# Splitting the weights of the first MLP product by two transfers from GpSimd instead of by ScalarE and VectorE

## The chip, the cores and the metric

The kernel runs on one core of one Trainium2 chip. The metric is the device time of one execution in microseconds; three runs of the kernel before gave 783.15 to 783.79 us, with a median of 783.71 us. Lower is better.

The engines are named as in the profile: PE is TensorE (PEld its weight loads), DVE is VectorE, ACT is ScalarE, POOL is GpSimd, SP is SyncE, which here only issues transfers. Each engine works through its own queue of instructions in order; engines wait for one another with semaphores.

## The reference

One transformer block on 512 tokens of width 1024 in float32: a gated linear attention branch and a latent attention branch, merged, projected and added to the input, and then an MLP with a squared ReLU, whose inner width is 4096. The part that the change touches is the first product of the MLP.

```
h = h + merged @ w_out[l]
m = rmsnorm(h, g_mlp[l])
h = h + jnp.square(jax.nn.relu(m @ w_ff1[l])) @ w_ff2[l]
return rmsnorm(h, g_final)
```

Here `m` is 512 x 1024, `w_ff1` is 1024 x 4096 and `w_ff2` is 4096 x 1024.

## The kernel before

**The products.** TensorE reads float32r operands, which hold fewer bits than float32. To keep the precision, each operand is split into `hi`, the value rounded to float32r, and `lo`, the rest `x - hi`. A product is then three matmuls onto the same accumulator (`mm3`, lines 91 to 93): hi by hi, lo by hi and hi by lo.

**The first MLP product.** The 4096 columns of `w_ff1` are cut into 32 blocks of 128 columns. The block is called f00 to f07 in quarter 0 of the MLP, f10 to f17 in quarter 1, up to f37. One block is 8 tiles of 128 x 128, laid out in SBUF as 128 partitions x 1024 numbers (512 KB). `hidden` multiplies a block with the normed and transposed rows `mT` in 24 matmuls of 512 columns: for each of the eight `k`, two that read the block's `hi` and one that reads its `lo`.

**How a block comes in.** `weights` (line 221) loads the block in float32 into a staging tile `wf` with one transfer from SP, in pieces of 512 bytes; ACT copies it, rounded, into `wh` (line 96); DVE writes `wl = wf - wh` (line 97). There are three staging tiles, four `wh` and four `wl`; a new block takes the buffer of the fourth one before it, once its last reader is through. These four pairs are shared with the weights of the second product.

**The order within a quarter.** A quarter has eight blocks of the first product, then seven block products with the quarter's part of `w_ff2` in a Strassen-like scheme (`ORDER`: 1, 5, 6, 3, 7, 4, 2). Each of these uses two pairs of `wh` and `wl` (`b1` to `b7`), made by the same `split`. In the order of taking buffers, a quarter goes: six blocks f, two tiles b1, blocks f6 and f7, two tiles each of b5, b6, b3, b7, b4 and b2. So f10 and f11 of the next quarter follow into the buffers of b4, f12 and f13 into those of b2, f14 and f15 into those of f10 and f11, the tiles of b1 into those of f12 and f13, f16 and f17 into those of f14 and f15, and b5 into those of f16 and f17.

**After a block.** ACT applies the ReLU (`fa`, line 1015) and the squares (`px`, `qx`); `pair_units` makes from two blocks the sums and differences of the left side and splits them on ACT and DVE (`ga`, `gb`, `gc`, `gd`).

**What sets the order on each engine.** A planner built into the framework orders the instructions of each engine by costs and dependencies of its own; the program forces an order only in some places (`in_program_order`, `goes_behind`). The first four blocks f00 to f03 are handled separately (`early`, and the branch for `j in (2, 3)`), so that they fit into the transition from the normed rows. POOL has nothing to do in the MLP except the last normalisation and one transfer from its queue, the gains `gfin` (line 1137).

Of the kernel before, what the change touches and what calls it, by code (L numbers as in the profile page):

```python
# [14 lines left out]
AF = mybir.ActivationFunctionType  # L15
ALU = mybir.AluOpType
AX = mybir.AxisListType

P = 128
S = 512  # L20
NT = S // P
D = 1024
KD = D // P
DFF = 4096
# [35 lines left out]
def tile_block(ctx: ExitStack, tc: tile.TileContext, t, out: bass.AP):  # L60
    nc = tc.nc
# [5 lines left out]
    def tl(shape, dt, tag, bufs, name):  # L67
        serial[0] += 1
        return sb.tile(shape, dt, tag=tag, bufs=bufs, name=f"{name}_{serial[0]}")

    def u2(name, dt=F32, shape=(P, S)):
        return tl(list(shape), dt, "u2", 25, name)
# [7 lines left out]
    def ps(tag, name):  # L80
        serial[0] += 1
        return pp.tile([P, S], F32, tag=tag, bufs=4, name=f"{name}_{serial[0]}")
# [4 lines left out]
    def raw(x):  # L87
        return x.bitcast(F32)

    def mm3(acc, lh, ll, rh, rl, start, stop, onto=False):  # L90
        nc.tensor.matmul(acc, lh, rh, start=start, stop=False, skip_group_check=onto)  # L91
        nc.tensor.matmul(acc, lh, rl, start=False, stop=False, skip_group_check=onto)  # L92
        nc.tensor.matmul(acc, ll, rh, start=False, stop=stop, skip_group_check=onto)  # L93

    def split(hi, lo, src, rest=nc.vector):
        nc.scalar.activation(hi, src, AF.Copy)  # L96
        rest.tensor_tensor(lo, src, raw(hi), op=ALU.subtract)  # L97
# [12 lines left out]
    def traced():  # L110
        return len(nc.cur_bb.bb.instructions)
# [15 lines left out]
    def goes_behind(late, early, engines):  # L127

        ins = nc.cur_bb.bb.instructions
        for e in engines:  # L130
            a, b = [[i for i in ins[x:y] if i.engine == e] for x, y in (early, late)]
            if a and b:
                issued_after(b[0], a[-1].name)
# [78 lines left out]
    def stage(nk, nw, name):  # L212
        wf = tl([P, nk, nw], F32, "wf", 3, f"{name}f")
        return wf

    def halves(nk, nw, name):
        wh = tl([P, nk, nw], F32R, "wh", 4, f"{name}h")
        wl = tl([P, nk, nw], F32R, "wl", 4, f"{name}l")
        return wh, wl

    def weights(src, name):
        k, w = src.shape
        nk = k // P
        wf = stage(nk, w, name)
        nc.sync.dma_start(wf, src.rearrange("(k p) w -> p k w", p=P))
        wh, wl = halves(nk, w, name)
        split(wh, wl, wf)
        return wh, wl

    w_in = t["w_in"][0]  # L230

    def proj_begin(w, col, name, tag="mm"):
        wh, wl = weights(w[:, col : col + P], name)
        return wh, wl, ps(tag, name)

    def proj_run(begun, src, half=None, ks=range(KD)):
        wh, wl, acc = begun
        c = slice(0, S) if half is None else slice(half * 256, half * 256 + 256)
        for k in ks:
            mm3(acc[:, c], wh[:, k, :], wl[:, k, :], src[k][:, 0, c], src[k][:, 1, c], k == 0, k == KD - 1)  # L240
        return acc
# [89 lines left out]
    for k in range(KD):  # L331
        wh, wl = (vh[k // 2][x][:, k % 2, :] for x in range(2))
# [173 lines left out]
    def gla_v(pr):  # L506

        accs = [ps("mm", f"gv{pr}{i}") for i in range(NT)]
        col = C_GV + pr * S
        res = v_tiles(pr)  # L510

        def piece(i, k2, wh, wl):
            tok = slice(i * P, (i + 1) * P)
            for kk in range(2):
                k = 2 * k2 + kk
                mm3(accs[i], xT[k][:, 0, tok], xT[k][:, 1, tok], wh[:, kk, :], wl[:, kk, :], k == 0, k == KD - 1)

        kept = []
        for k2 in range(KD // 2):
            wh, wl = weights(w_in[k2 * 2 * P : (k2 + 1) * 2 * P, col : col + S], f"gv{pr}{k2}")  # L520
            if k2 >= 2:
                kept.append((k2, wh, wl))
                continue
            for i in range(NT):
                piece(i, k2, wh, wl)
        for i in range(NT):
            for k2, wh, wl in kept:
                piece(i, k2, wh, wl)
            v_evict(accs[i], res[i], i)
        return res  # L530
# [329 lines left out]
    def rows_product(lhs, w, nk, name, first_done, done, flip):  # L860
        for c in range(2):
# [11 lines left out]
            for k2 in range(nk // 2):  # L873
                wh, wl = weights(w[k2 * 2 * P : (k2 + 1) * 2 * P, c * S : (c + 1) * S], f"{name}{c}{k2}")
                if k2 >= nk // 2 - staggered:
                    kept.append((k2, wh, wl))
                    continue
                for i in range(NT):
                    piece(i, k2, wh, wl)
# [32 lines left out]
    mT = fm.out  # L912
    w1, w2 = t["w_ff1"][0], t["w_ff2"][0]
# [33 lines left out]
    FQ = DFF // P // NQ  # L947
# [55 lines left out]
    def hidden(qd, j):  # L1003

        if qd == 0 and j < 2:
            acc = early[j][2]
        elif qd == 0 and j in (2, 3):
            at = traced()
            begun = proj_begin(w1, j * P, f"f{qd}{j}")
            goes_behind((at, traced()), span["norm", NT - 1] if j == 2 else span["evacuate", 1], SPLITTERS)  # L1010
            acc = proj_run(begun, mT)
        else:
            acc = proj_run(proj_begin(w1, (qd * FQ + j) * P, f"f{qd}{j}"), mT)
        a = u2(f"fa{qd}{j}")
        nc.scalar.activation(a, acc, AF.Relu)  # L1015
        return a

    def pair_units(qd, p, a22):

        px, qx = u2(f"px{qd}{p}"), u2(f"qx{qd}{p}")  # L1020
        for x in range(2):
            a = hidden(qd, 2 * p + x)
            c = slice(x * HT, (x + 1) * HT)
            nc.scalar.activation(px[:, c], a[:, 0:HT], AF.Square)  # L1024
            nc.scalar.activation(qx[:, c], a[:, HT:S], AF.Square)
        a11, a12, a21, a22_ = px[:, 0:HT], px[:, HT:S], qx[:, 0:HT], qx[:, HT:S]
        y, z = u2(f"y{qd}{p}"), u2(f"z{qd}{p}")
        s1, s2, s3, s4 = y[:, 0:HT], y[:, HT:S], z[:, 0:HT], z[:, HT:S]
        g1 = u4(f"ga{qd}{p}")
        split(g1[:, 0, :], g1[:, 1, :], px)  # L1030
        nc.vector.tensor_tensor(s1, a21, a22_, op=ALU.add)
        nc.vector.tensor_tensor(s2, s1, a11, op=ALU.subtract)  # L1032
        nc.vector.tensor_tensor(s3, a11, a21, op=ALU.subtract)
        nc.vector.tensor_tensor(s4, a12, s2, op=ALU.subtract)
        h2, l2 = u2(f"gbh{qd}{p}", F32R), u2(f"gbl{qd}{p}", F32R)
        split(h2, l2, y)
        h3, l3 = u2(f"gch{qd}{p}", F32R), u2(f"gcl{qd}{p}", F32R)
        split(h3, l3, z)
        c4 = slice((p % 2) * HT, (p % 2 + 1) * HT)
        split(a22[:, 0, c4], a22[:, 1, c4], a22_)  # L1040
        lo, hi = slice(0, HT), slice(HT, S)
        return {1: (g1[:, 0, lo], g1[:, 1, lo]), 2: (g1[:, 0, hi], g1[:, 1, hi]),
                5: (h2[:, lo], l2[:, lo]), 6: (h2[:, hi], l2[:, hi]),
                7: (h3[:, lo], l3[:, lo]), 3: (h3[:, hi], l3[:, hi]),
                4: (a22[:, 0, c4], a22[:, 1, c4])}
# [148 lines left out]
```

## Time and profile before

| what | value |
|---|---|
| median of three runs | 783.71 us |
| the profiled execution | 783.52 us, of which the span is 781.8 us |
| PE busy | 772.8 us (99%) |
| DVE busy | 544.2 us (70%) |
| ACT busy | 410.1 us (52%) |
| POOL busy | 104.1 us (13%) |
| the MLP on the span | blocks f00 on from 444.6 us; each quarter some 82 us |

The span runs from the first to the last instruction; what lies around it is 1.7 us in the profiled execution. In the views, a row of a timeline starts with the instruction's start and its duration in microseconds, followed by its engine, line, operation and `out<-in`. Buffer numbers are left out of the names, so the tiles of b1, b5 and so on of one quarter all show as `b_10h`. A matmul's shown duration holds its passage through the array, so the starts of two matmuls in a row, not the duration, tell the rate. A group's row gives the busy time, the mean duration in nanoseconds and the idle time just before, with what ended it.

### The profile page before, as it was taken

To read this page: it belongs to the slowest core of one execution; us is meant where nothing else is said; L and a number is where in the kernel's file an instruction comes from. 1 tells how busy PE (TensorE), PEld (TensorE's weight loads), DVE (VectorE), ACT (ScalarE), POOL (GpSimd) and SP (SyncE) were. 2 spreads that over 40 slices of the span, in tenths; PEclk is the share of its full clock that TensorE was granted. 3 is DMA by queue.
4 is the path that set the end of the run, shared out by engine and by line. 5 is a ranking of instruction groups with operands and counts; after the bars stand their busy time and mean duration, and the time that the engine had idled before them with its cause. 6 is when DMAs were issued, how large, how long until landed. Compare 5 with 4: busy or idle time off the path is not lost.

```text
span 781.8 us, 10005 instructions
## 1 busy us (share of the span) xinstructions
PE 772.8 (99%) x3736; PEld 648.5 (83%) x3736; DVE 544.2 (70%) x839; ACT 410.1 (52%) x685; POOL 104.1 (13%) x168
## 2 busy tenths in 40 slices
PE   9999999999999999999999999999999999999996
PEld 7888888888888888888888898888888888888885
DVE  7767656576566449799973578874787578848695
ACT  7564624532562236798853366435553455436644
POOL 1023203213021314211120100000000000000014
PEclk9999999999999999999999999999999999999998
DMA  7634133133223411523033731155106411460002
GB/s 247 168 90 111 33 84 106 54 94 107 62 75 82 75 40 51 139 55 108 28 128 88 267 110 54 53 179 145 43 14 208 141 46 35 162 183 6 28 1 108
DMA packets 102385, 74.47 MB, mean 95 GB/s; under 512 B 14976, under 2 KB 86656, under 8 KB 102336
## 3 DMA queue, kind: packets, MB, share of 16 engines
q1 hardware_dynamic: 101248, 70.66, 31.4%
q10 hardware_dynamic: 864, 2.38, 0.8%
q0 software_dynamic: 224, 0.79, 0.3%
q8 instruction: 29, 0.48, 0.3%
q14 instruction: 20, 0.16, 0.1%
HBM read 69.62 MB, written 2.10 MB: 92 GB/s over the span
## 4 chain that ended last, share of the span: by engine, by line
PE 94%; issue 3%; DVE 2%; ACT 1%; POOL 0%; POOLq 0%
PE f L92 8%; PE f L93 7%; PE f L91 7%; PE gx L91 4%; PE gx L93 4%; PE gx L92 4%; PE gv L320 3%; PE gr L91 2%; PE gr L93 2%; PE wo L93 2%; PE wo L91 2%; PE gr L92 2%; PE gz L93 2%; PE za L92 2%; PE gz L91 2%
## 5 line engine op out<-in xcount | busy, mean ns | idle before, releaser
L962 DVE TENSOR_TENSOR w<-w,w 128x1024 f32<-128x1024 f32 x32 | 38.7, 1220 | 0.4
L1137 POOL DMA_DIRECT2D gfin<-in_g_final x1 | 0.7, 653 | 282.6 <-PE f L93 282.6
L744 ACT ACTIVATE e<-s,top 128x512 f32<-128x512 f32 x32 | 21.9, 685 | 6.0 <-DVE top L741 5.0
L909 DVE TENSOR_TENSOR h<-gx,h 128x512 f32<-128x512 f32 x32 | 21.5, 683 | 1.8 <-PE gx L93 1.7
L97 DVE TENSOR_TENSOR pT<-tp,pT 128x512 fp32r<-128x512 f32 x32 | 21.6, 678 | 0.5 <-ACT pT L96 0.4
L741 DVE TENSOR_REDUCE top<-s 128x1 f32<-128x512 f32 x32 | 21.6, 678 | 0.1
L96 ACT ACTIVATE pT<-tp 128x512 fp32r<-128x512 f32 x32 | 18.9, 593 | 3.1 <-PE tp L758 2.9
L758 PE MATMUL tp<-ident,e 128*128 128x128 f32 x128 | 19.2, 273 | 0.1
L91 PE MATMUL av<-pT,v 128*128 128x256 f32 x64 | 19.3, 301 | 0.0
L776 POOL TENSOR_TENSOR tb<-tb,g 128x512 f32<-128x512 f32 x8 | 11.1, 1383 | 56.9 <-DVE tb L775 43.8
L758 PEld LDWEIGHTS tp<-ident,e 128*128 128x128 f32 x128 | 15.3, 140 | 3.9 <-DVE pT L97 0.5
L535 DVE TENSOR_TENSOR za<-za,R 128x512 f32<-128x512 f32 x8 | 5.5, 691 | 18.7 <-PE za L93 18.7
L1015 ACT ACTIVATE fa<-f 128x512 f32<-128x512 f32 x32 | 18.5, 578 | 0.0
L92 PE MATMUL av<-pT,v 128*128 128x256 f32 x64 | 18.4, 288 | 0.0
L93 PE MATMUL av<-pT,v 128*128 128x256 f32 x64 | 18.1, 283 | 0.0
L96 ACT ACTIVATE gbh<-y 128x512 fp32r<-128x512 f32 x16 | 10.1, 634 | 14.0 <-DVE y L1032 14.0
L451 POOL TENSOR_TENSOR qk<-qkf,e3f 128x256 f32<-128x256 f32 x8 | 7.8, 973 | 63.8 <-DVE qkf L443 63.8
L91 PE MATMUL s<-kbuf,q 128*128 128x512 f32 x32 | 13.7, 429 | 0.3 <-DVE pT L97 0.3
L1024 ACT ACTIVATE px<-fa 128x256 f32<-128x256 f32 x32 | 13.4, 418 | 1.0
L96 ACT ACTIVATE b_20h<-w 128x1024 fp32r<-128x1024 f32 x7 | 7.4, 1059 | 12.1 <-PE gx L93 6.0
L96 ACT ACTIVATE b_10h<-w 128x1024 fp32r<-128x1024 f32 x7 | 7.4, 1059 | 12.1 <-PE gx L93 6.0
L96 ACT ACTIVATE b_00h<-w 128x1024 fp32r<-128x1024 f32 x7 | 7.4, 1058 | 12.1 <-PE gz L93 6.0
(1460 smaller groups left out, 2806.9 us busy)
## 6 DMA issues: line engine op xcount, KB each, us to landing
w<-in_w_ff SPq DMA_DIRECT2D x64, 256.0 KB, 3.4
x<-in_xt SPq DMA_DIRECT2D x8, 256.0 KB, 5.3
vw<-in_w_in SPq DMA_DIRECT2D x8, 256.0 KB, 5.4
q<-ro SPq DMA_DIRECT2D x16, 128.0 KB, 4.6
h<-in_x ACTq DMA_DIRECT2D x4, 512.0 KB, 4.9
out<-ms SPq DMA_DIRECT2D x7, 256.0 KB, 2.2
gr0f<-in_w_in SPq DMA_DIRECT2D x1, 512.0 KB, 5.6
za0f<-in_w_in SPq DMA_DIRECT2D x1, 512.0 KB, 6.5
```

The costliest lines, as they stand in the source:

```text
L91: nc.tensor.matmul(acc, lh, rh, start=start, stop=False, skip_group_check=onto)
L92: nc.tensor.matmul(acc, lh, rl, start=False, stop=False, skip_group_check=onto)
L93: nc.tensor.matmul(acc, ll, rh, start=False, stop=stop, skip_group_check=onto)
L96: nc.scalar.activation(hi, src, AF.Copy)
L97: rest.tensor_tensor(lo, src, raw(hi), op=ALU.subtract)
L320: nc.tensor.matmul(v_accs[i], a[:, i * P : (i + 1) * P], b, start=k == 0 and x == 0, stop=k == KD - 1 and x == 2)
L741: nc.vector.tensor_reduce(top, acc, axis=AX.X, op=ALU.max, negate=True)
L744: nc.scalar.activation(e, acc, AF.Exp, bias=top, accum_out=tot)
L758: nc.tensor.transpose(tp[:, k * P : (k + 1) * P], e[:, k * P : (k + 1) * P], ident)
L909: nc.vector.tensor_tensor(hc, acc, hc, op=ALU.add)
L962: nc.vector.tensor_tensor(wq[dst][g], wq[x][g], wq[y][g], op=op)
L1015: nc.scalar.activation(a, acc, AF.Relu)
```

## The change

For the 28 blocks from f04 on, `hidden` no longer calls `weights`. A new function makes `wh` and `wl` with two transfers issued by POOL and one ACT instruction. The first transfer reads the float32 block and writes it into the float32r tile `wh`, rounded on the way. ACT writes `-wh` into `wl`. The second transfer reads the same float32 block again and adds it to what stands in `wl`, so that `wl` becomes `w - wh`. The staging tile, the rounding copy on ACT and the subtraction on DVE are gone for these blocks. The blocks are laid out on the host so that each partition's 1024 numbers lie in one run of 4 KB.

```
-            acc = proj_run(proj_begin(w1, (qd * FQ + j) * P, f"f{qd}{j}"), mT)
+            name = f"f{qd}{j}"
+            wh, wl = weights_by_transfer(t["w1_blocks"][qd * FQ + j].rearrange("p (k f) -> p k f", k=KD), name)
+            acc = proj_run((wh, wl, ps("mm", name)), mT)
...
+    def weights_by_transfer(src, name):
+
+        wh, wl = halves(KD, P, name)
+        nc.gpsimd.dma_start(wh, src)
+        nc.scalar.activation(wl, raw(wh), AF.Copy, scale=-1.0)
+        nc.gpsimd.dma_start(wl, src, accum_op=ALU.add)
+        return wh, wl
...
+    arrays["w1_blocks"] = np.ascontiguousarray(
+        arrays["w_ff1"][0].reshape(KD, P, DFF // P, P).transpose(2, 1, 0, 3).reshape(DFF // P, P, D)
+    )
```

## The prediction

> **What bounds the kernel now.** I read the page first (parts 1 and 2), then busy times by stage, then single instructions of TensorE and ScalarE around one quarter of the MLP, then the transfers.
>
> ```profile
> span 781.8 us, 10005 instructions
> ...
> PE 772.8 (99%) x3736; PEld 648.5 (83%) x3736; DVE 544.2 (70%) x839; ACT 410.1 (52%) x685; POOL 104.1 (13%) x168
> ...
> PE   9999999999999999999999999999999999999996
> ...
> PEclk9999999999999999999999999999999999999998
> ```
> ```profile
> core 0: us, PE busy (x) PEld busy (x) DVE busy (x) ACT busy (x) POOL busy (x), PEclk, DMA share, GB/s
> ...
> 458.00:500.00 42.00, 42.00 (x187) 34.46 (x186) 33.02 (x48) 27.88 (x50) 0.00 (x0) 1.00 0.22 63
> 500.00:536.00 36.00, 36.00 (x161) 29.80 (x160) 25.45 (x30) 13.99 (x14) 0.00 (x0) 1.00 0.57 174
> ```
> PE is busy in every slice, and in the stages of the MLP it is busy the whole time (42.00 of 42.00 us) at full clock, with DVE and ACT below it and the transfers at 0.22 and 0.57 of their time. The MLP is bound by TensorE alone. The change takes no matmul away, so taking work from DVE, ACT or SP can bring nothing there; the only question is whether the new way of making the weights is late.
>
> ```profile
> 529.34 0.39 PE L91 MATMUL f<-mT,f10h 128*128 128x512 f32 x1
> ...
> 551.10 0.39 PE L91 MATMUL f<-mT,f14h 128*128 128x512 f32 x1
> ...
> 556.54 0.39 PE L91 MATMUL f<-mT,f15h 128*128 128x512 f32 x1
> ```
> From f14 to f15 are 24 matmuls in 5.44 us: 0.227 us each.
>
> ```profile
> 522.74 1.06 ACT L96 ACTIVATE f10h<-f10f 128x1024 fp32r<-128x1024 f32 x1 [3.02 <-DMA w<-in_w_ff]
> 524.10 1.06 ACT L96 ACTIVATE f11h<-f11f 128x1024 fp32r<-128x1024 f32 x1 [0.30 <-PE gx L93]
> 528.18 1.06 ACT L96 ACTIVATE f12h<-f12f 128x1024 fp32r<-128x1024 f32 x1 [3.02 <-PE gw L93]
> 529.54 1.06 ACT L96 ACTIVATE f13h<-f13f 128x1024 fp32r<-128x1024 f32 x1 [0.30 <-PE gw L93]
> ...
> 556.52 1.06 ACT L96 ACTIVATE f16h<-f16f 128x1024 fp32r<-128x1024 f32 x1 [0.74 <-PE f L92]
> ...
> 562.92 0.58 ACT L1015 ACTIVATE fa<-f 128x512 f32<-128x512 f32 x1
> ...
> 566.69 0.63 ACT L96 ACTIVATE gch<-z 128x512 fp32r<-128x512 f32 x1
> ```
> ```profile
> L97 DVE TENSOR_TENSOR f14l<-f14f,f14h 128x1024 fp32r<-128x1024 f32 x1 | 1.2, 1226 | 3.6 <-ACT f14h L96 3.6
> ```
> These rows show when a buffer comes free, since the split waits for that alone (its release is PE). Counted from f10's first matmul (T = 529.34), the buffer of f10 is free at -6.6, of f11 at -5.2, of f12 at -1.2, of f13 at +0.2 us. That of f16 comes free as f15 begins. A split then needs 1.06 + 1.23 us and fits each time, because the float32 block waits in a staging tile.
>
> **The change part by part.** Gone are 28 rounding copies on ACT (in their place 28 negating copies of the same shape, so 1.06 us each), 28 subtractions on DVE (28 x 1.23 = 34 us of an engine that is not the bound) and 28 issues on SP. All three lay beside PE: 0. What was hidden was the load itself; now the load may only start when the buffer `wh` is free, and the chain is buffer free, first transfer, ACT 1.06 us, second transfer, matmul. New on POOL are 56 transfers. The order of the changed kernel's instructions on POOL in quarter 1 is:
>
> ```
> f10h f11h f10l f12h f11l f13h f12l f14h f13l f14l f15h f15l f16h f16l f17h f17l
> ```
> ```profile
> gfin<-in_g_final POOLq DMA_DIRECT2D x1, 512.0 KB, 3.9
> pos_i<-in_positions POOLq DMA_DIRECT2D x1, 256.0 KB, 4.4
> ```
> ```profile
> wo12f<-in_w_out SPq DMA_DIRECT2D x1, 512.0 KB, 3.5
> ...
> f10f<-in_w_ff SPq DMA_DIRECT2D x1, 512.0 KB, 4.2
> ...
> f35f<-in_w_ff SPq DMA_DIRECT2D x1, 512.0 KB, 5.7
> ```
> ```profile
> w<-in_w_ff SPq DMA_DIRECT2D x64, 256.0 KB, 3.4
> ```
> ```profile
> L1065 POOL TENSOR_TENSOR ms<-h,gfin x4: 1292/1302/2162, 760.0 to 766.6; 128x512 f32<-128x512 f32 x4
> ...
> L1137 POOL DMA_DIRECT2D gfin<-in_g_final x1: 653/653/653, 732.3 to 732.3; - x1
> ```
> POOL is held 0.65 us by an issue of this shape. Call the first transfer's issue to landing `a`, the second's `c`. For `a`: between 3.5 (wo12f) and 5.7 (f35f, among other loads); nearest are gfin, the same shape from the same queue, at 3.9, and f10f at 4.2. I take 4.2; that rounding on the way costs more is not excluded. For `c` there is no adding transfer in the trace. It must read the block and the target: at least a plain 4.2, at most two plain ones in a row, 8.4. Twice the bytes (256 to 512 KB) went from 3.4 to 4.2, 0.8 us per 256 KB, so a second reading of 512 KB adds 1.7: I take c = 5.9. Ends kept: a + c from 7.0 to 12.8, taken 10.1.
>
> The Trainium skill, page "Collectives: The Full Stack", section "The bandwidth ceiling: the fold count and why AG ≠ RS ≠ AR", says that an adding transfer is slow by its two source reads on one ring, at half the rate, and not by the addition; doubling the whole landing by it would give c = 8.4 and a sum at the upper end below. No run here shows it yet.
>
> Handovers get 0.1 us (an allowance).
>
> *Start of quarters 1, 2, 3 (S1).* f10h issues at -6.6 and lands at a - 6.6; ACT is done at a - 5.44; f10l lands at a + c - 5.34, PE sees it at a + c - 5.24. Until then PE has only four matmuls (two of f10's `hi`, two of f11's), to 0.91. S1 = a + c - 6.15 = 3.95 us. f11l follows within f10's 5 us, and f12h, queued behind f10l, has f10 and f11 to hide under. f13l is queued behind f14h, which waits until f10 is through at c + 4.0; it lands at 2c + 4.6 and is needed at c + 14.85, late only from c = 10.3. f14 and f15 have three blocks (16 us) of lead.
>
> *f6 of each quarter, four times (S2).* Its buffer comes free as f15 begins (call it 0). f16l lands at a + c + 1.26, is seen at a + c + 1.36. PE has f15's 24 matmuls, two of f16 and nine of product 1 that the planner put there: 35 x 0.227 = 7.94. S2 = a + c - 6.58 = 3.52 us. For f06 the same holds.
>
> *f7 (S3).* f17h is issued behind f16l, at a + 1.9; ACT is busy with ReLU to `gch` (562.92 to 567.32, 4.4 us) from f15's end to 9.95, the landing is at 2a + 1.9 = 10.3, so f17l is seen at 2a + c + 3.3. PE gets there at a + c + 7.7. S3 = a - 4.4: nothing at 4.2, but nothing to spare.
>
> f04 is late only from c = 6 or so (issued near 463.6, needed near 469.6). gfin now stands behind f37l on POOL; it went out at 732.3 and is read at 760.0, which covers it.
>
> *Product 1 after f7.*
> ```profile
> 493.44 0.39 PE L93 MATMUL gx<-b_00h,ga 128*128 128x512 f32 x1
> 493.79 0.50 PE L91 MATMUL gx<-b_01h,ga 128*128 128x512 f32 x1
> ```
> ```profile
> L962 DVE TENSOR_TENSOR w<-w,w 128x1024 f32<-128x1024 f32 x32 | 38.7, 1220 | 0.4
> ```
> Already before, the matmul that needs f07's left side came 0.12 us late. With nine to thirteen of product 1's matmuls spent as filler, the planner now puts b6's copy (1.06 us) and one L962 addition (1.22 us) ahead of that left side: 0 to 1.2 us each quarter; I take 0.5, 2 us in all.
>
> *The clock.*
> ```profile
> 774.98 0.28 PE L93 MATMUL gend<-b_31h,ga 128*128 128x256 f32 x1
> ```
> ```profile
> 777.00:777.50 0.50, 0.00 (x0) 0.00 (x0) 0.31 (x1) 0.31 (x1) 0.16 (x1) 1.00 0.39 143
> 777.50:778.00 0.50, 0.00 (x0) 0.00 (x0) 0.45 (x1) 0.41 (x1) 0.00 (x0) 0.81 1.00 373
> 778.00:778.50 0.50, 0.00 (x0) 0.00 (x0) 0.00 (x0) 0.00 (x0) 0.00 (x0) 0.50 1.04 389
> ...
> 780.00:782.00 2.00, 0.00 (x0) 0.00 (x0) 0.00 (x0) 0.00 (x0) 0.00 (x0) 0.50 0.10 38
> ```
> PE ended at 775.26 and the granted clock fell to 0.50 at about 777.8, after 2.5 us of idleness, and stayed there for the 4 us left. S1 and S2 are longer than that. How long the clock stays down once PE works again no row shows; at 0 to 4 us a stall costs 0 to 1.9 more, 0 to 13 for seven. I take 5, since the stalls pass 2.5 us by only 1 to 1.5.
>
> The Trainium skill, page "TensorE: Matmul & The Clock Gate", section "Part 1: The HAM clock gate (the "warmup" mystery)", has the clock halved after an idle window of about 3.4 us and full again after a busy one. By that a stall that trips it costs 1.7 us, 12 for seven. The trace agrees on the half, after 2.5 us here.
>
> *Sum.* 3 x 3.95 + 4 x 3.52 + 2 + 5 = 33 us on the profiled execution's 783.5 us (0.2 below the median of the runs): 816.5 us, 4% slower.
>
> **The rivals.**
> (1) Fast transfers: a + c between 6.4 and 9. At the fastest 512 KB row for both (7.0), S1 = 0.85, S2 = 0.42, together 4.2, no clock term: 788. At 9.0: 8.6 + 9.7 + 2 = 20, 804. For it: quiet 3.5 us landings, and runs of 4 KB instead of 512 bytes. Against: gfin's 3.9 in such runs. At 3.2 us for each, S1 is 0.25, S2 nil: 784 to 786. The Trainium skill gives such a 3.2 by its fit of 2.0 us plus bytes over 436 GB/s ("DMA: Bandwidth & Descriptors", section "Anatomy of one DMA — SWDGE (gpsimd) path"); gfin's 3.9 disagrees.
> (2) The adding transfer is a slow path, c over 9: then PE waits a plain transfer longer in all seven places, f13l is late too, and the clock falls each time. At c = 12: 30 + 39 + 5 (three times 1.8 at f13) + 2 + 13 = 89 us, 872. For it: nothing of the kind in the trace bounds it. Against: the transfers are idle half the time or more.
> (3) Not slower: the chain is hidden. That needs a + c below 6.15, so both transfers in some 3.1 us, below any 512 KB row; then 783 to 785, and only the 0.5 per product 1 is left.
> That the first transfer does not round would leave the queues and the traffic as they are, so no other time.
>
> **How the numbers follow.** Forecast (a + c from 9 to 12.8; 800 to 845): 0.62. Fast (785 to 800): 0.18. Slow path (above 845): 0.17. Not slower: 0.03. The range of 790 to 850 leaves out the lower part of the fast case and most of the slow one. Runs of this kernel differ by some 0.1%, so 0.2% (1.6 us) is about what can be told from none. Faster 0.01, same 0.02, slower 0.97.
>
> **What would show it.** Seven gaps on PE: ahead of the third matmul of f10, f20, f30 and of f06, f16, f26, f36 (released by a transfer), each a + c less 6.2 to 6.6; f17 without one. ACT's copies at L234 released by a transfer, with DVE some 34 us less busy. Landing times of the `h` and `l` transfers on POOL's queue give a and c directly. The forecast is wrong if f14 or f04 wait too, if PE stays dense, or if the matmuls after a gap run at 0.227 us although the gap passed 2.5 us.

## The result, and the profile after

The changed kernel takes 836.45 us (median of four runs, 834.23 to 839.74) beside 783.62 us for the kernel before in the same session: a ratio of 1.068, 95% interval 1.064 to 1.072. It is 53 us slower; the forecast was 33. The profiled execution, which the readings below are taken from, is the longest of the four, 839.74 us.

The page of the changed kernel, its span, busy times, and the slices of PE and of its clock:

```profile
span 838.0 us, 10055 instructions
...
PE 791.2 (94%) x3736; PEld 655.8 (78%) x3736; DVE 510.6 (61%) x811; ACT 409.5 (49%) x685; POOL 145.4 (17%) x224
...
PE   9999999999999999999999979798898989979896
...
PEclk9999999999999999999999999999998989989998
```

The number of matmuls is the same, 3736. Against before (span 781.8, PE 772.8) the span grew by 56.2 us, and the page splits that without any model: PE is idle for 838.0 - 791.2 = 46.8 us where it was idle for 9.0, so 37.8 us are waits; and the same matmuls are busy for 18.4 us longer, which points at the clock. DVE lost its 34 us, as forecast, and nothing came of it.

Where PE waits, in the chain of waits of the changed kernel (in each row: us in total, times, longest):

```profile
PE gx L91 <- DVE h L917: 6.4, 4, 1.6
PE f L93 <- DMA f10l<-in_w_blocks: 5.0, 1, 5.0
PE f L93 <- DMA f30l<-in_w_blocks: 4.8, 1, 4.8
PE f L93 <- DMA f20l<-in_w_blocks: 4.1, 1, 4.1
PE f L93 <- DMA f26l<-in_w_blocks: 3.4, 1, 3.4
PE f L93 <- DMA f36l<-in_w_blocks: 3.0, 1, 3.0
PE f L93 <- DMA f06l<-in_w_blocks: 2.9, 1, 2.9
PE f L93 <- DMA f16l<-in_w_blocks: 2.7, 1, 2.7
PE f L93 <- DMA f17l<-in_w_blocks: 1.9, 1, 1.9
...
PE f L93 <- DMA f07l<-in_w_blocks: 1.4, 1, 1.4
PE gx L91 <- ACT ga L96: 0.5, 1, 0.5
...
PE f L93 <- DMA f37l<-in_w_blocks: 0.3, 1, 0.3
```

The seven forecast gaps are the seven longest single waits, each released by the adding transfer. Two kinds of wait were not in the forecast sum: f7 (f17, f07, f37), put there at nothing, and four waits for DVE's line 917. The rows sum to 36.4 of the 37.8 us.

The transfers of quarter 1 on POOL's queue (the last number is issue to landing in us):

```profile
f10h<-in_w_blocks POOLq DMA_DIRECT2D x1, 512.0 KB, 5.2
...
f10l<-in_w_blocks POOLq DMA_DIRECT2D x1, 512.0 KB, 5.6
...
f11l<-in_w_blocks POOLq DMA_DIRECT2D x1, 512.0 KB, 9.2
f13h<-in_w_blocks POOLq DMA_DIRECT2D x1, 512.0 KB, 10.0
...
f16h<-in_w_blocks POOLq DMA_DIRECT2D x1, 512.0 KB, 3.8
f16l<-in_w_blocks POOLq DMA_DIRECT2D x1, 512.0 KB, 5.5
f17h<-in_w_blocks POOLq DMA_DIRECT2D x1, 512.0 KB, 6.7
f17l<-in_w_blocks POOLq DMA_DIRECT2D x1, 512.0 KB, 5.4
```

A rounding transfer that is alone lands in 3.8 us (f16h), an adding one in 5.4 to 5.6. A transfer that goes out beside an adding one is drawn out: f17h, issued 0.56 us behind f16l, needs 6.7, and of the four issued within 1.8 us around f10l and f11l two need 9.2 and 10.0.

### The clock in the profile after

The timeline of PE in the changed kernel at f10, the first long gap (in brackets the idle time before, and what ended it):

```profile
537.71 0.39 PE L92 MATMUL f<-mT,f11h 128*128 128x512 f32 x1
543.08 0.79 PE L93 MATMUL f<-mT,f10l 128*128 128x512 f32 x1 [4.98 <-DMA f10l<-in_w_blocks]
543.67 0.63 PE L91 MATMUL f<-mT,f10h 128*128 128x512 f32 x1
544.10 0.63 PE L92 MATMUL f<-mT,f10h 128*128 128x512 f32 x1
```

After the gap the matmuls start 0.43 us apart instead of 0.227. Steps of half a microsecond over the same stretch (columns: window, its length, busy time of PE, PEld, DVE, ACT and POOL, the granted clock, the transfers' share, GB/s) show the clock fall within the first step and come back at the end of it all:

```profile
543.00:543.50 0.50, 0.42 (x1) 0.42 (x2) 0.00 (x0) 0.00 (x0) 0.00 (x0) 0.62 0.71 221
...
546.50:547.00 0.50, 0.50 (x3) 0.40 (x3) 0.00 (x0) 0.11 (x1) 0.09 (x1) 0.96 0.99 287
```

By the shares of 1.00 and 0.50 in the first and last row it was down from 543.1 to 546.5, 3.4 us. The same happens near 591, 639, 680, 738 and 779 us, for 3.4 us each in three of the six places and 6.8 us in the other three: 30.7 us at half speed. The mean granted clock of the core, 0.979, tells the same: 0.021 x 838 = 17.6 us of lost clock, half of 30.7 and 2.4 after the last matmul. But a slow clock costs only while PE has work, and PE still stood waiting for 3.7 of these 30.7 us. It was busy for 27.0, so half speed cost some 13.5 us. The other 4.9 of the 18.4 us are not worked out one by one; part of them is only how the trace counts, since the last matmul before a gap shows its whole 0.39 us and not 0.227 (by an estimate, 2.4 us for the 15 waits of the rows above).

The falls lie at whole multiples of 3.41 us from one another (543.1 and 590.9 are 14 of them apart). So I cut the stretch around f16 and f17 into such windows, in the same columns:

```profile
587.50:590.90 3.40, 1.47 (x7) 0.92 (x6) 2.45 (x2) 2.01 (x4) 0.00 (x0) 1.00 0.69 135
590.90:594.30 3.40, 3.40 (x9) 2.63 (x10) 0.00 (x0) 0.00 (x0) 0.00 (x0) 0.50 0.00 0
577.25:580.66 3.41, 2.19 (x9) 1.24 (x7) 2.48 (x7) 2.40 (x7) 0.73 (x2) 1.00 0.76 114
580.66:584.07 3.41, 1.92 (x8) 1.61 (x9) 1.25 (x2) 0.70 (x2) 0.00 (x0) 1.00 0.62 193
```

At f17 PE was idle for 1.9 us only, but all of it lay in one window, which was busy for 1.47 of 3.40 us (43%): the clock fell at its end. At f16 PE was idle for 2.7 us, spread over two windows that were 64% and 56% busy: the clock stayed at 1.00. So in these windows it is the share of busy time that goes with the fall, not the length of one gap.

The rest of the trace agrees. The windows ahead of the six falls were busy for 0% to 43%; every other window of the MLP at full clock, up to the one in which PE ends, was busy for 53% or more (604.56 to 607.98 us: 53%), and the clock stayed. The profiles of all thirteen kernels, cut in the same way from one of their falls (from 30 us on), put the bound near a half: after a window below 44% the clock always fell, between 44% and 50% it did either, and above 50% it fell once (five pairs, at 326 us, far ahead of the MLP, after a window of 65%). The same windows tell why a fall lasts 3.4 or 6.8 us. Where the first slow window was at least 84% busy, the clock was back after it (here at 779 us: 91%); where it was at most 82% busy, because PE's wait went on into it, the clock stayed down for another (here 64%, 55% and 82% at 639, 680 and 738 us).

The Trainium skill, page "TensorE: Matmul & The Clock Gate", section "Part 1: The HAM clock gate (the "warmup" mystery)", has a free-running window of 3413 ns, and asks for an idle window before the clock falls. The spacing agrees with the trace (47.8 us for 14 windows); that the window must be idle does not, since one that was 43% busy was enough here.

### The profile page after: what moved, and what is told of

The parts are those of the page before. It is cut to its first block, busy times and chain, and to the rows that moved or that the text cites. A ratio compares the mean times of both kernels' runs of the same rounds, so it can differ in the third digit from the quotient of the medians.

```text
span 838.0 us, 10055 instructions
## 1 busy us (share of the span) xinstructions
PE 791.2 (94%) x3736; PEld 655.8 (78%) x3736; DVE 510.6 (61%) x811; ACT 409.5 (49%) x685; POOL 145.4 (17%) x224
## 5 line engine op out<-in xcount | busy, mean ns | idle before, releaser
L1041 DVE TENSOR_TENSOR y<-qx 128x256 f32<-128x256 f32 x16 | 6.7, 421 | 74.6 <-ACT qx L1035 74.6
L1025 ACT ACTIVATE fa<-f 128x512 f32<-128x512 f32 x32 | 18.6, 582 | 5.1 <-PE f L93 5.0
L96 ACT ACTIVATE gbh<-y 128x512 fp32r<-128x512 f32 x16 | 10.1, 631 | 18.7 <-DVE y L1042 18.7
L92 PE MATMUL av<-pT,v 128*128 128x256 f32 x64 | 18.4, 288 | 0.0
L97 DVE TENSOR_TENSOR b_20l<-w,b_20h 128x1024 fp32r<-128x1024 f32 x7 | 8.5, 1221 | 15.9 <-ACT b_20h L96 15.9
L93 PE MATMUL av<-pT,v 128*128 128x256 f32 x64 | 18.1, 283 | 0.0
L97 DVE TENSOR_TENSOR b_30l<-w,b_30h 128x1024 fp32r<-128x1024 f32 x7 | 9.0, 1281 | 13.2 <-ACT b_30h L96 13.2
L543 DVE TENSOR_TENSOR za<-za,R 128x512 f32<-128x512 f32 x8 | 5.5, 691 | 18.4 <-PE za L93 18.4
L97 DVE TENSOR_TENSOR b_10l<-w,b_10h 128x1024 fp32r<-128x1024 f32 x7 | 8.5, 1220 | 13.3 <-ACT b_10h L96 13.3
```

## The experiments

Each of them is timed against the kernel before on the same chip and in the same session (783.2 to 783.6 us there); ratios are to that kernel, with their 95% intervals. I went part by part, then by cause. The theory is that of the prediction: a chain of buffer free, rounding transfer, negating copy, adding transfer, with PE waiting for its end.

**The block layout alone** (loads from SP and split as before):

```
     def weights_by_transfer(src, name):
         wh, wl = halves(KD, P, name)
-        nc.gpsimd.dma_start(wh, src)
-        nc.scalar.activation(wl, raw(wh), AF.Copy, scale=-1.0)
-        nc.gpsimd.dma_start(wl, src, accum_op=ALU.add)
+        wf = stage(KD, P, name)
+        nc.sync.dma_start(wf, src)
+        split(wh, wl, wf)
```

> Only the layout in blocks of the changed kernel is kept; the blocks come in by SP into the staging tile and are split by ACT and DVE as before. Theory (the time comes from the chain of two transfers behind a free buffer): within 0.2% of before, 783 to 784.5 us, no gap on PE at f10 or f16. Rival (the layout or the rows of 4 KB matter by themselves): more than 2 us away from before.

Measured: 783.07 us, ratio 0.9994 (0.9985 to 1.0003). The layout costs and brings nothing, as a kernel bound by PE says.

**The rounding transfer alone** (DVE subtracts, from a staged block, as before):

```
         nc.gpsimd.dma_start(wh, src)
-        nc.scalar.activation(wl, raw(wh), AF.Copy, scale=-1.0)
-        nc.gpsimd.dma_start(wl, src, accum_op=ALU.add)
+        nc.vector.tensor_tensor(wl, wf, raw(wh), op=ALU.subtract)
```

(with the staged load of `wf` by SP ahead of it)

> Of the changed kernel only the first transfer is kept: POOL's transfer makes wh, rounded; the block also comes by SP into a staging tile, and DVE subtracts as before. The chain behind a free buffer is then one transfer (4 to 5 us) and 1.23 us on DVE, some 6.3 us. Theory: f10, whose buffer is free 6.3 us ahead, and f16, with 5.4 us and two matmuls, are late by 0 to 1 us: 784 to 791 us. Rival (a transfer from POOL or its rounding hurts by itself): above 810 us.

Measured: 784.62 us, ratio 1.0012 (1.0002 to 1.0022); PE has no wait above 0.4 us in the MLP. Its f16h lands in 3.8 us, like that of the changed kernel. One transfer behind the buffer's release still fits where the split did; this half of the change is free, or nearly.

**The adding transfer alone** (ACT writes `wh` and then `-wh`, from a staged block):

```
-        nc.gpsimd.dma_start(wh, src)
+        wf = stage(KD, P, name)
+        nc.sync.dma_start(wf, src)
+        nc.scalar.activation(wh, wf, AF.Copy)
```

> Of the changed kernel only the second transfer is kept: the block comes by SP into a staging tile, ACT makes wh from it and -wh, POOL's adding transfer makes wl. The chain is 1.06 + 1.06 + 5.5 us and handovers, some 8 us. Theory: gaps of 0.7 to 1.2 us at f10, f20, f30 and of up to 2 us at f06 to f36, no fall of the clock: 787 to 798 us. Rival (the adding transfer alone is the cause): above 815 us.

Measured: 812.5 us, ratio 1.0374 (1.0355 to 1.0394). That misses my expectation and is close to the rival's 815. PE waits 3.4, 3.1 and 3.0 us at f10, f20 and f30 and 2.0 to 2.7 us at the four blocks f6, 18.6 us in all, and is busy for 10.1 us longer than before; the clock, which I had expected to stay up, falls five times. The transfers of this kernel at the start of quarter 1:

```profile
f10l<-in_w_blocks POOLq DMA_DIRECT2D x1, 512.0 KB, 8.1
f14f<-in_w_blocks SPq DMA_DIRECT2D x1, 512.0 KB, 7.6
f11l<-in_w_blocks POOLq DMA_DIRECT2D x1, 512.0 KB, 9.9
...
f16l<-in_w_blocks POOLq DMA_DIRECT2D x1, 512.0 KB, 5.6
```

Alone the adding transfer takes 5.6 us here too, but f10l, which PE waits for, goes out together with others and needs 8.1. I had priced every adding transfer as if it were alone. The two halves by themselves cost 1.0 and 28.9 us; together they cost 53. That fits a chain in which one stands behind the other, where the time of the first is no longer hidden.

**Copying in place of adding.** The second transfer overwrites `wl` with the weight; the addition is left out, everything else stays:

```
-        nc.gpsimd.dma_start(wl, src, accum_op=ALU.add)
+        nc.gpsimd.dma_start(wl, src)
```

> The changed kernel with a second transfer that copies instead of adding, so that wl holds the weight itself and not the rest, and the result is not the reference's. Order and waits are those of the changed kernel. Theory: an adding transfer lands 1.3 us later than a copying one, so each of the gaps at f10, f6 and f7 is 1 to 1.4 us shorter and the clock falls less often: 815 to 826 us. Rival (adding is the main cost): 785 to 800 us. Rival (adding costs nothing): 834 to 840 us.

Measured: 809.99 us, ratio 1.0337 (1.0318 to 1.0357): 26 us, half of the loss, come from adding rather than copying. That is more than I expected and less than the rival had it. The transfers of f16 and f17, in this kernel:

```profile
f16h<-in_w_blocks POOLq DMA_DIRECT2D x1, 512.0 KB, 3.9
f16l<-in_w_blocks POOLq DMA_DIRECT2D x1, 512.0 KB, 4.0
f17h<-in_w_blocks POOLq DMA_DIRECT2D x1, 512.0 KB, 4.7
f17l<-in_w_blocks POOLq DMA_DIRECT2D x1, 512.0 KB, 4.0
```

So adding costs 1.4 to 1.5 us on the transfer itself, and 2.0 us on the one that stands beside it (f17h, 6.7 to 4.7). With f17h on time the waits at f7 are gone, and the shorter gaps spare the clock: PE is busy for 780.6 us in a span of 809.3. Against the changed kernel (791.2 in 838.0) the span is 28.7 us shorter; 18.1 of these are waits that are gone, and 10.6 are the clock and what goes with it.

**A fifth pair of buffers**, and its control. To make room, the staging tiles go from three to two and another pool from 25 to 23; the control has these two and keeps four pairs.

```
-        return tl(list(shape), dt, "u2", 25, name)
+        return tl(list(shape), dt, "u2", 23, name)
...
-        wf = tl([P, nk, nw], F32, "wf", 3, f"{name}f")
+        wf = tl([P, nk, nw], F32, "wf", 2, f"{name}f")
...
-        wh = tl([P, nk, nw], F32R, "wh", 4, f"{name}h")
-        wl = tl([P, nk, nw], F32R, "wl", 4, f"{name}l")
+        wh = tl([P, nk, nw], F32R, "wh", 5, f"{name}h")
+        wl = tl([P, nk, nw], F32R, "wl", 5, f"{name}l")
```

> The changed kernel with five pairs of wh and wl instead of four; room for it is made by two staging tiles instead of three and 23 instead of 25 tiles of the u2 pool. Theory: f10 now takes the buffer of the last tile of b7, free 10.9 us before the quarter ends, and f16 that of f13, one block earlier; the chain of some 11 us is hidden, so the gaps at f10, f16 and f17 go, the clock stays at 1.00, and it is some 50 us faster than the control with four pairs, 784 to 797 us depending on what the smaller pools cost. Rival (the two transfers or the POOL queue cost time whatever the lead): stays above 820 us.

> Control for the run with five pairs: the changed kernel with two staging tiles and 23 u2 tiles, but four pairs. Both theories: like the changed kernel, 834 to 850 us, with the same seven large gaps; whatever is above 836 us is the price of the smaller pools in the stages ahead of the MLP.

Measured: 818.19 us with five pairs, ratio 1.0438 (1.0424 to 1.0452); the control 836.76, ratio 1.0672 (1.0657 to 1.0687), like the changed kernel. So an earlier release brings 18.6 us, and my theory that the release is all fell: 35 us are left, near the rival's 820 us. In the MLP alone it brings more. With five pairs the first matmul of f00 starts at 450.2 us, in the control at 446.1, and in the changed kernel at 444.9; from there to the end of the span are 366.4 us with five pairs and 389.4 in the control. The fifth pair thus wins 23 us in the MLP and loses 4 ahead of it, where PE has three waits of 0.8 to 1.3 us that the control does not have. Why the order ahead of the MLP changes was not tried. The gaps at f10, f20 and f30 shrink to 0.6, 1.8 and 0.6 us, but f16 and f36 now wait for 4.1 and 4.2. The timeline of this kernel on POOL:

```profile
560.17 0.56 POOL L233 DMA_DIRECT2D f16h<-in_w_blocks  x1 [4.06 <-PE f L93]
570.18 0.85 POOL L235 DMA_DIRECT2D f16l<-in_w_blocks  x1 [9.45 <-ACT f16l L234]
570.74 0.87 POOL L233 DMA_DIRECT2D f17h<-in_w_blocks  x1
```

POOL stands for 9.45 us ahead of f16l, waiting for ACT's negating copy. ACT had that copy behind others in its order and ran it only at 568.85:

```profile
568.31 0.63 ACT L96 ACTIVATE gbh<-y 128x512 fp32r<-128x512 f32 x1 [3.99 <-DVE y L1042]
568.85 1.04 ACT L234 ACTIVATE f16l<-f16h 128x1024 fp32r<-128x1024 f32 x1
```

f16h had landed at 564.0 (3.8 us after its issue); from 564.3 on ACT sat for 3.99 us in front of `gbh` with the copy queued behind it, and f17h stands behind f16l on POOL though it waits for nothing else. The lost time has moved from the release to the order on two queues.

**The negating copy on DVE**, with five pairs and with four:

```
-        nc.scalar.activation(wl, raw(wh), AF.Copy, scale=-1.0)
+        nc.vector.tensor_scalar(wl, raw(wh), -1.0, None, op0=ALU.mult)
```

> The run with five pairs (818.19 us), with the negating copy of the rounded half on DVE instead of ACT; POOL's order of issue is unchanged. Theory (what is left with five pairs is ACT's order: the copy for f16 ran some 4.6 us after its rounded half had landed, and f17's two transfers stand behind it on POOL): the gaps of TensorE at f16, f36 and f26 (4.11, 4.22 and 2.50) fall below 1 each and those behind them on the queue with them, 803 to 810 us. Rival (the transfers themselves are too long, each after the other on one queue, whoever copies): the gaps stay at their places and the time within 3 us of 818.

> The changed kernel (836.45 us) with the negating copy on DVE instead of ACT. Theory (with four pairs the chain waits for a buffer to come free and for the two transfers; who copies matters little): 830 to 838 us, gaps at the same seven places. Rival (ACT's order is the larger part of the chain): 815 to 825.

Measured: 809.94 us with five pairs, ratio 1.0346 (1.0322 to 1.0370), and 830.39 with four, ratio 1.0601 (1.0585 to 1.0617): 8 and 6 us less. Both times are in the theory's ranges. With four pairs the gaps are at the seven places, as it had them, and the four waits for line 917 shrink from 1.6 to 0.7 us each. With five pairs the gaps are not as it had them: f16 fell from 4.1 to 1.4 us, while f36 kept 3.0, f26 rose to 3.1 and f17 from 1.0 to 2.5, so there the time came out right by luck. On POOL, f16l still goes out 7.3 us after f16h:

```profile
560.71 0.56 POOL L233 DMA_DIRECT2D f16h<-in_w_blocks  x1 [5.24 <-PE f L93]
568.02 0.86 POOL L235 DMA_DIRECT2D f16l<-in_w_blocks  x1 [6.75 <-DVE f16l L234]
```

Now POOL waits for DVE's copy instead, 6.75 us. Taking the copy off ACT is worth 6 to 8 us; that DVE's order takes some of ACT's place is read from these two rows, and no run isolates it.

**Five pairs and a copying second transfer** (again without the addition):

> The run with five pairs (818.19 us), whose second transfer copies the weight into the low half instead of adding it (the low half is then the weight itself, so this part of the computation is left out). With four pairs the same edit took 26 us off (836.45 to 809.99). Theory (adding costs through its longer transfers and those that it slows, and a fifth pair does not hide it): the gaps at f16 and f36 halve, 795 to 805 us. Rival (five pairs already hide the adding, and what is left is order alone): 812 to 818.

Measured: 790.97 us, ratio 1.0086 (1.0069 to 1.0103), below the range that I gave. The longest waits of this kernel in the MLP:

```profile
PE f L93 <- DMA f20l<-in_w_blocks: 1.1, 1, 1.1
PE f L93 <- DMA f10l<-in_w_blocks: 1.0, 1, 1.0
```

Two more, at f37 and f36, are of 0.8 and 0.7 us; no other block is waited for.

Four runs make a square (us):

| | adding | copying | difference |
|---|---|---|---|
| four pairs | 836.45 | 809.99 | 26.5 |
| five pairs | 818.19 | 790.97 | 27.2 |
| difference | 18.3 | 19.0 | |

The two prices add up: about 27 us for adding instead of copying, about 19 for the release of the fourth buffer, and 8 for what both leave. Of the last, most lies ahead of the MLP: in the profile with five pairs and copying, f00 starts at 450.1 us where it started at 444.6 before.

**Matmuls to keep the clock up.** Sixteen matmuls without use go onto the accumulator of f10, f20 and f30 before these begin (the first real one starts it afresh):

```
+            if qd and j == 0:
+                at = traced()
+                for _ in range(16):
+                    nc.tensor.matmul(acc, mT[0][:, 0, 0:P], mT[0][:, 0, :], start=True, stop=True)
+                goes_behind((at, traced()), (last_pe[0], at), PE_ONLY)
```

> The changed kernel with 16 matmuls of 512 columns of no use at the start of quarters 1, 2 and 3, between the last matmul of product 2 and the first of f10, f20, f30 (the first real matmul overwrites what they leave). They fill 3.6 us of a gap of 4.1 to 5.0 us. Theory (time at half clock is lost on top of the gaps): no fall of the clock at f10, f20, f30, which cost 1.7 + 3.4 + 3.4 us in the profiled execution, so 826 to 831 us. Rival (what runs slowly there only shortens later waits): 834 to 840 us as without them.

Measured: 839.55 us, ratio 1.0721 (1.0692 to 1.0751), not faster. Half of what I wanted happened: at f10 the gap is 1.1 us, and the granted clock stays at 1.00 across it:

```profile
540.00:541.00 1.00, 0.46 (x3) 0.04 (x1) 0.00 (x0) 0.00 (x0) 0.00 (x0) 1.00 0.94 193
```

But the planner's order on POOL came out otherwise (f13l now ahead of f14h, which f15 follows), and PE waits elsewhere, with the clock falling behind the new waits:

```profile
PE f L93 <- DMA f25l<-in_w_blocks: 4.4, 1, 4.4
PE f L93 <- DMA f15l<-in_w_blocks: 4.1, 1, 4.1
```

The time is in the rival's range, but as the order changed with it, the run decides neither way and gives no price for the clock. That some 13.5 us go with it is worked out from the trace of the changed kernel, and no run isolates it.

**DVE's addition first.** The four waits for line 917 stand ahead of product 6, which goes on in the accumulators of product 1: DVE must have added product 1 to the rows before. The edit prepares product 6's second operand behind product 1, so that DVE takes the addition first:

```
-            if ahead and not behind:
+            if ahead and not behind and m != 1:
...
-            if behind:
+            if behind or m == 1:
```

> The changed kernel, with the preparation of b6 placed behind product 1, and DVE forced to take the addition of product 1 to the rows ahead of b6's. In the changed kernel PE waits 1.6 us in each quarter for that addition, before product 6. Theory (the planner's order on DVE is the cause): these four waits go, 828 to 832 us. Rival (DVE has too much to do there): the wait moves to b6's own split, 834 to 840 us.

Measured: 842.09 us, ratio 1.0737 (1.0712 to 1.0762), so this theory fell. The waits for line 917 are gone from the list. In their place PE waits for the operands of product 6, 1.0 us for ACT's copy and 1.0 for DVE's half behind it, in each of the four quarters (2.0 for the 1.6 before):

```profile
PE gx L91 <- ACT b_00h L96: 1.0, 1, 1.0
...
PE gx L92 <- DVE b_10l L97: 1.0, 1, 1.0
```

Whichever comes first, PE arrives at product 6 before its operands are split and the addition is done. With five pairs, and with the adding transfer alone, this wait does not occur; with the copying transfer and four pairs it does (four times 1.6), and with four pairs and DVE's negating copy it is four times 0.7. Both of its conditions, the addition and the split, follow on the late blocks f6 and f7; which step would cure it stays open.

None of these versions beats the kernel before; the best is the block layout alone, which equals it.

## Why the prediction was right, and where it was not

The time fell into the forecast case, at its upper end, and the mechanism is the one named. Term by term, in us:

| term | predicted | measured |
|---|---|---|
| start of quarters 1 to 3 (S1) | 11.9 | 13.9 |
| f6 of four quarters (S2) | 14.1 | 12.0 |
| f7 (S3) | 0 | 3.6 |
| product 1 and what follows it | 2 | 6.9 |
| clock | 5 | 13.5, in 18.4 us of busier PE |
| sum | 33 | 56.2, with the 18.4 and 1.4 of smaller waits |

*S1 and S2* hold, with their formulas: S2 at f16 is a + c - 6.58 with a = 3.8 and c = 5.5, so 2.7, and 2.7 was measured; S1 at f10 with 5.2 and 5.6 is 4.65, and 5.0 was measured. `c` was taken as a plain landing and 1.7 for a second reading of 512 KB; 3.8 against 5.5 is 1.7. That the two terms together come out at 25.9 for 26.0 is luck in part: `a` was taken as 4.2 everywhere, and was 4.5 to 5.2 at f10, f20 and f30 and 3.8 to 4.9 at the blocks f6, and `c` as 5.9 where it was 5.4 to 5.6, so that S1 was too low by about as much as S2 was too high. The row that gave f10's buffer as free at -6.6 shows a release by a transfer and not, as the prediction says, by PE. The changed kernel bears the figure out all the same: PE's release lets POOL issue f10h at 530.70 us, 6.3 us ahead of f10's first matmul.

The Trainium skill, page "Collectives: The Full Stack", section "The bandwidth ceiling: the fold count and why AG ≠ RS ≠ AR", gives the adding step of a reduce-scatter, which reads two sources, half the rate of an all-gather; doubling the whole landing, which the prediction had weighed, would make 7.6 of f16h's 3.8, and f16l took 5.5. The rows show 1.7 us more and not a doubled landing; that the second reading is what costs them no run shows by itself.

*S3* was mis-sized. It used the same `a` for f17h as for a transfer that is alone. Behind f16l on the queue f17h took 6.7, and a - 4.4 gives 2.3 where 1.9 was measured; f07h took 6.3, which gives 1.9 for 1.4. The text said "nothing to spare"; the neighbour took it. The copying run shows that it is the adding in the neighbour: 4.7, and no wait. The formula does not hold where the clock fell just before. f27h and f37h took 6.3 too, but PE waited 0 and 0.3 us at these blocks. There the clock was at half speed after the gaps at f26 and f36 (679.7 to 686.5 us and 778.6 to 782.1 us), PE came to f7 later, and the transfer was in time. So the terms of the sum do not simply add: a slow clock takes up part of the next wait.

*Product 1* was wrong in its place. I expected the left side of f7 to be late, and PE waited 0.5 us once for that. The waits came one product later, at the addition of product 1 to the rows, a step that I had not listed.

*The clock* is the largest miss. From the end of the kernel before I had read that the clock falls 2.5 us after PE goes idle, and took the seven gaps as just past that. The windows above show another rule: f17's 1.9 us tripped it, f16's 2.7 and f06's 2.9 did not. So that a matmul should run slow after every gap above 2.5 us, which I had named as a test, failed at f16 and f06. Where it fell, it stayed for one or two whole windows, up to 1.7 us lost in each, and the 13.5 us in all are just past the upper end of the 0 to 13 that I kept.

*Costs taken as nothing* were nothing: the layout (0.9994), and the rounding transfer with its issues on POOL (1.0012 with 28 of the 56). f04, f13 and f14 did not wait, as worked out; f04, priced as late from a c of 6, had 5.8, and in the run with four pairs and DVE's copy, where f04l took 7.1, PE did wait for it, 1.4 us. The rival with the slow adding path had the gaps too long, but the thing it stood on was partly real: crowded, these transfers need 8 to 10 us, though seldom where PE waits for them.

## What to carry to other kernels

Where one engine is busy for 99%, work taken from the others brings nothing (here 34 us of DVE's), and each load that must now wait for its final buffer is a risk: a staging tile is what lets a load run ahead of the release. When a load becomes a chain of two transfers and a copy, count each link in the order of its queue, with the landing time that it has beside its neighbours, not alone. Sum PE's gaps by windows of the clock as well as by length: at f17 a gap of 1.9 us that fell into one window of 3.4 us cost 1.7 us more.

## What the runs showed of the hardware that I had not expected

- A transfer from float32 into a float32r tile takes hardly longer than one that leaves float32 as it is: for 512 KB, 3.8 us in the changed kernel (f16h) beside 3.8 for `gfin` from the same queue, and in the run with the rounding transfer alone 3.8 (f16h) beside 3.6 for the same block in float32 from SP (f16f).
- An adding transfer of 512 KB into SBUF lands in 5.4 to 5.6 us when it is not crowded (f16l, f17l, f26l, f27l), against 4.0 for the copying f16l, and it slows what runs beside it: f17h took 6.7 us behind an adding transfer and 4.7 behind a copying one.
- The clock of PE fell after a window of 3.4 us that was 43% busy, and did not after windows that were 53%, 56% and 64% busy. Over all profiles the bound lies between 44% and 50%, but for one fall after 65%; the busy share that the trace gives does not tell it more sharply. A fallen clock came back after the first window that was at least 84% busy, and not after one of 82%.
